# A one-core decoder layer: another order on VectorE around w_o, and two small fetches at another place

## The chip, the core and the metric

The kernel runs on one core of one Trainium2 chip. A core has five engines that run side by side, each through its own list of instructions in order, and that wait for one another by semaphores. TensorE (PE in the profile) does matrix products, and the loading of its stationary operand is shown beside it as PEld. VectorE (DVE) and ScalarE (ACT) do elementwise work, and read the results of TensorE from PSUM banks. GpSimd (POOL) does some elementwise work and starts some transfers. SyncE (SP) starts most transfers between the device's memory and the on-chip memory. The metric is device time in microseconds (us) for one launch.

## The reference

One pre-norm layer on 512 tokens of 1024 features, in float32. What matters here is the middle and the end of it:

```
merged = gates[0] * y_a + gates[1] * y_b + gates[2] * y_c      # y_c = ssd_mixer(...) @ w_c
x = x + merged @ w_o                                           # w_o is 1024 x 1024
u = rmsnorm(x, ln2_g)          # x * rsqrt(mean(x*x) + 1e-6) * ln2_g, row by row
h = causal_dwconv(u @ w_up, conv_w, conv_b)                    # w_up is 1024 x 5632, three taps
x = x + (silu(h[:, :2816]) * h[:, 2816:]) @ w_down
out = rmsnorm(x, final_g)
```

The norm ahead of the FFN needs a whole row of the new x before any of its 1024 features can be used, and every product of w_up needs the normed rows. The convolution's taps and bias (`ffn_conv_w`, `ffn_conv_b`) are needed as columns, one scalar for each feature.

## The kernel before

**Arithmetic.** Each float32 product is done as three products of a reduced format: an operand is split in a high part and a rest, `high` and `low`. For a weight tile, ScalarE casts the high part (`wh`, line 195) and VectorE subtracts it from the raw tile to get the rest (`wl`, line 217, the "weight sum" below is this instruction and its relatives on line 1377). `mm3` (line 238) then issues high by high, high by low and low by high.

**Jobs.** The work is a list of jobs (`program`), each with a weight tile to fetch (`fetch`, on SP), to cast (`cast`) and to split (`low`), and a `body` that issues the products. While the body of job n runs, job n+1's tile is split, job n+2's is cast and job n+3's is fetched. Small pieces of other work are generators in the list `running`; `step()` lets each of them go on by one `yield`, so where a `step()` stands in a body decides where such a piece stands in the lists of the engines. The lists of PE, ACT, DVE and POOL are in the order in which the Python code issues the instructions; that of SP is set by the framework.

**w_o.** `wo_group` computes `merged @ w_o` by seven products of half size in place of eight, so seven jobs named two, five, three, one, six, seven and four, in this order. Each job makes two products, one for each of two blocks of 128 rows, in two PSUM banks (`bank[0]`, `bank[1]`). Banks called A serve one, six, seven and four, banks called B two, five and three: a later job of the same banks adds onto what an earlier one left. So after each product `read(i)` has VectorE add the bank to a tile of x (line 1351, "a reading of a bank"), and the next job that adds onto this bank can't start its product before that reading. Job one finishes the left half of row blocks 0 and 1, job six their right half, job seven the left-out half of row blocks 2 and 3, and job four the rest of these.

**The norm.** Behind a reading stands either `first` or `then`. `first` (after one's readings, and after seven's) begins the norm of a row block with the half that is ready: the squares and their sum on ScalarE (line 439), two small VectorE instructions that make `v0` and `vh` from the sum (lines 463 and 1297), and the product with the norm's gain on GpSimd (line 464). `then` (after six's and four's readings) takes the other half: squares and a square root on ScalarE (line 473), a small VectorE instruction (line 478), and after a `yield` the reciprocal and its refinement on VectorE (lines 481 to 483), then the two halves of the normed rows `u`, one on VectorE (line 487), one on ScalarE (line 488). `norm_turn` transposes the normed rows on PE into PSUM (line 453, `uT`), and ScalarE and VectorE make the high part `uh` and the rest `ul` of them (lines 456 and 457). For row blocks 0 and 1 this last part runs as `rest(2)` in `running`; for row blocks 2 and 3 it is called from the first FFN jobs (`opening`, line 1543), which therefore start on row blocks 0 and 1 alone.

**Small tables.** `ff_cols` fetches the convolution's taps and bias as rows (three transfers on line 512), transposes them on PE (line 518, `fcol0p` and `fcol1p`) and copies the result with VectorE (line 519, `fcol`). It is called after job one (`i == 3`), and the PE and VectorE part runs at the third `step()` after it. The transposes of `ff_cols` and `norm_turn` take PSUM banks in turn from one set of four. ScalarE's square root needs a table that is loaded when the function is first used after another set (an ACT_TABLE_LOAD on line 473). `load_x1` fetches the norm's gain and some tiles of x ahead of the fourth of the four w_c jobs; `one_read` holds what follows one's readings, among it job four's weight sum (`total`, line 1377).

Of the kernel before, what the change touches and what calls it, by code (L numbers as in the profile page):

```python
# [10 lines left out]
F32 = mybir.dt.float32  # L11
F32R = mybir.dt.float32r
AF = mybir.ActivationFunctionType
OP = mybir.AluOpType
AX = mybir.AxisListType

P = 128
S = 512
D = 1024
KD = D // P  # L20
EPS = 1e-6
# [61 lines left out]
def trunk(ctx: ExitStack, tc, out, x, rel_bias, ln1_g, w_in, b_gate, w_a, pool_w, pool_scale, w_b,  # L83
# [3 lines left out]
    act, dve, pool, pe, sp = nc.scalar, nc.vector, nc.gpsimd, nc.tensor, nc.sync  # L87
# [5 lines left out]
    cpool = ctx.enter_context(tc.tile_pool(name="const", bufs=1))  # L93
# [12 lines left out]
    def T(name, dt=F32, shape=(P, S)):  # L106
        return big.tile(list(shape), dt, name=name, tag="t")
# [7 lines left out]
    def small(name, shape, dt=F32):  # L115
        return tiny.tile(list(shape), dt, name=name, tag="tiny")
# [4 lines left out]
    eps = cpool.tile([P, 1], F32, name="eps")  # L121


    waiting, running = [], []
# [38 lines left out]
    def after(n, it):  # L163
        for _ in range(n):
            yield
        yield from it
# [269 lines left out]
    def squares(eng, src, ss):  # L436
        junk = T("junk")
        if eng is act:
            act.activation(junk, src, AF.Square, accum_out=ss)
        else:  # L440
            dve.scalar_tensor_tensor(junk, src, 1.0, src, OP.mult, OP.mult, accum_out=ss)

    def grow(src):
        g = [T("grow") for _ in range(2)]
        for h in range(2):
            sp.dma_start(g[h], src[h * S:(h + 1) * S].partition_broadcast(P))
        return g

    def norm_turn(us, uh, ul, tb):
        for h in range(2):  # L450
            ps = SM("uT")
            for j in range(4):
                pe.transpose(ps[:, j * P:(j + 1) * P], us[h][:, j * P:(j + 1) * P], eye)
            pv = ps.rearrange("p (j t) -> p j t", j=4)
            hh = uh[:, 4 * h:4 * h + 4, tb * P:(tb + 1) * P]
            act.copy(hh, pv)
            dve.tensor_sub(ul[:, 4 * h:4 * h + 4, tb * P:(tb + 1) * P], pv, hh.bitcast(F32))

    def norm_early(t, g, h=0):

        ss, v0, xg = small("ss", [P, 1]), cpool.tile([P, 1], F32, name=f"v0_{len(V0)}"), T("xg")
        squares(act, t, ss)
        dve.tensor_scalar(v0, ss, 1.0 / D, EPS, OP.mult, OP.add)
        pool.tensor_tensor(xg, t, g[h], OP.mult)
        V0.append(v0)
        return v0, xg
# [788 lines left out]
    X1 = {}  # L1255
    nxt = {}
    late, late_split = [], []

    def load_x1():
        nxt["g2"] = grow(ln2_g[0])  # L1260
        for tb, h in ((0, 1), (1, 1), (2, 0), (3, 0)):
            t = X1[tb, h] = T("x1")
            sp.dma_start(t, x[tb * P:(tb + 1) * P, h * S:(h + 1) * S])

    def wo_group():
# [26 lines left out]

        def first(tb, h):
            half = 1 - h
            v0, xg = norm_early(X1[tb, half], nxt["g2"], half)
            vh = cpool.tile([P, 1], F32, name=f"vo{tb}")
            dve.tensor_scalar(vh, v0, -0.5, None, OP.mult)
            nxt[tb] = v0, vh, xg

        def then(tb, h):  # L1300
            if "uh" not in nxt:
                nxt["uh"] = upool.tile([P, KD, S], F32R, name="uh2", tag="uh")
                nxt["ul"] = upool.tile([P, KD, S], F32R, name="ul2", tag="ul")
            v0, vh, xg0 = nxt[tb]
            us = [T("u0"), T("u1")]
            it = norm_late(X1[tb, h], nxt["g2"], v0,
                           lambda: (us[h], (us[1 - h], xg0)), vh, h, True)
            next(it)

            def rest(n=1):  # L1310
                next(it, None)
                for _ in range(n):
                    yield
                norm_turn(us, nxt["uh"], nxt["ul"], tb)

            if tb < 2:
                running.append(rest(2))
            elif tb == 2:
                r2 = rest()
                next(r2)  # L1320
                late.append(r2)
            else:
                late.append(rest())
                for _ in late_split.pop(0):
                    pass
# [50 lines left out]
        def total(out, a, b, op=OP.add):  # L1376
            dve.tensor_tensor(out, a, b, op)
            return out

        def one_read(tb):  # L1380
            first(tb, 1)
            if tb == 0:
                total(four.raw, four.raw, W[2])

        two = job("A12", quarter(1, 0), None, B, (0, 0), apart=True, fresh=True)
        five = job(1, None, lambda: W[0], B, (1, 1), apart=True, fresh=True)
# [226 lines left out]
    def program():  # L1613
        yield from jobs_a(w_in, C_POOL, 8, uhk, ulk, KD, pool_evac)
        yield Call(lambda: waiting.append(rows_of_bias()))
        yield from v_jobs(0)
        yield Call(lambda: running.extend(after(3 * p, sums_of_u(p)) for p in (0, 1)))
        yield from qk_jobs(0)
        yield from pool_out_job()
        yield Call(lambda: attend(0))  # L1620
        yield Call(lambda: waiting.insert(3, ssd_prep()))
        gates = gate_seven(1)
        pair, residues_of_v = v_pair()
        groups = gates, pair, qk_sevens(1)
        for i, job in enumerate(branch_jobs(1, w_b, YB, 8, more=range(7))):
            if i == 1:
                yield Call(gates.load[0])
            if i == 2:
                yield Call(lambda: running.extend(after(2 * p - 4, sums_of_u(p)) for p in (2, 3)))
                yield Call(gates.load[1])  # L1630
                yield Call(gates.load[2])
            yield job
        yield Call(lambda: second_table())
        last = None
        for group, next_ in zip(groups, groups[1:] + (None,)):
            yield group.two
            if last:
                yield last.four
            last = group
            for i, job in enumerate(group.jobs):  # L1640
                if next_ and i >= 2:
                    yield Call(next_.load[i - 2])
                yield job
        xbc = jobs_a(w_in, C_XBC, 12, uhk, ulk, KD, xbc_evac)
        yield next(xbc)
        yield last.four
        yield Call(lambda: attend(1))
        yield Call(lambda: running.extend(after(2, f()) for f in (residues_of_v, residues_of_bias)))
        yield from xbc
        yield Call(ssd_start)  # L1650
        yield from qk_jobs(2)
        yield Call(lambda: attend(2))
        yield Call(lambda: fill([after(2, combine())]))
        yield from gate_jobs(0)
        many = {"a": branch_jobs(0, w_a, AO, 3), "g": gate_jobs(2),
                "Z": z_jobs(0), "z": z_jobs(1)}
        load, sums, group = wo_group()
        for token in MIX:
            if token == "w":
                yield Call(load)  # L1660
            elif token in many:
                yield next(many[token])
            else:
                yield Call(lambda i=int(token): waiting.append(y_norm(i)))
        yield Call(finish)
        for i, job in enumerate(branch_jobs(2, w_c, YT, 8, last=True)):
            if i == 1:
                yield Call(sums)
            if i == 3:
                yield Call(load_x1)  # L1670
            yield job
        for i, job in enumerate(group):
            yield job
            if i == 3:
                yield Call(ff_cols)
        loads, groups = zip(*(down_group(base) for base in range(0, KS, 8)))
        between = {}
        for group, ats in zip(groups, AT):
            for jobs_, at in zip(group, ats):
                between.setdefault(at, []).extend(jobs_)  # L1680
        for i, job in enumerate(up_jobs()):
            yield job
            for load, ats in zip(loads, AT):
                if i == ats[0] - 3:
                    yield Call(load)
            yield from between.get(i, ())
        yield Call(lambda: fin.setdefault("g", grow(final_g)))
        plain = down_jobs(0)
        yield next(plain)
        yield from between.get(2 * (KF // 2), ())  # L1690
        yield from plain
        yield from down_jobs(1)
# [22 lines left out]
    first = [MM("pa") for _ in range(4)]  # L1715
# [63 lines left out]
    for tb in range(2):  # L1779
        s0, s1, v, sq, r, rt = (small(n, [P, 1]) for n in ("s0", "s1", "v", "sq", "r", "rt"))  # L1780
# [25 lines left out]
    ss = row_squares(2, small("ss", [P, 4]), 2)  # L1806
# [36 lines left out]
    n = 0  # L1843
# [68 lines left out]
```

## Time and profile before

| what | us |
|---|---|
| median of 3 runs | 1023.51 (1023.18 to 1023.67) |
| profiled execution, its own time | 1024.06 |
| span of that execution in the trace | 1022.3 |
| PE busy | 1007.1 |
| DVE busy | 718.6 |
| ACT busy | 518.7 |
| POOL busy | 143.7 |

The profile's times count from the start of the span. Job one of w_o starts on PE at 633.17 us, the first FFN job at 664.28, and from 677.52 the FFN runs over all rows. A row of the timeline gives the start, the length, the engine, the line, the operation, the tiles written and read, the count of merged instructions, and in square brackets the engine's idle time before it and what ended that. PEclk is the clock that TensorE was granted, 1.00 being full speed.

### The profile page before, as it was taken

The page shows a single profiled execution, that of the slowest core. Times are in us where ns is not written, and L with a number is a line of the kernel's source. Part 1 is how long each engine was busy: PE and PEld are TensorE (multiplying, and loading weights), DVE is VectorE, ACT ScalarE, POOL GpSimd, SP SyncE. Part 2 cuts the span into 40 slices and gives each one's busy share as a digit, 9 for nine tenths or more (in the row PEclk, how much of TensorE's full clock was granted, in tenths as well). Part 3 has the DMA queues.
Part 4 walks back from the last instruction along what each step waited for, and adds up shares of the span by engine and source line. Part 5 has one row for each costly group of instructions (what it writes and reads, how often), then busy time and mean ns, then how long its engine had stood idle before and what let it go on. Part 6 is the DMA issues. An engine that isn't in the chain of part 4 may idle for free.

```text
span 1022.3 us, 13624 instructions
## 1 busy us (share of the span) xinstructions
PE 1007.1 (99%) x5378; PEld 858.1 (84%) x5378; DVE 718.6 (70%) x910; ACT 518.7 (51%) x877; POOL 143.7 (14%) x128
## 2 busy tenths in 40 slices
PE   8999999999999999999999999899999999999997
PEld 8898878999988888888888887698888888888885
DVE  6564768677757647667889688658778768685756
ACT  5433546564435476879567235554444444433434
POOL 1691000010000000000064501102111100111002
PEclk9999999999999999999999999999999999999999
DMA  8538222155253343552256346332232332321322
GB/s 269 169 100 210 95 72 76 57 150 167 93 183 107 90 126 102 145 142 86 83 166 166 113 145 162 129 118 89 95 112 83 99 107 82 125 83 42 124 103 83
DMA packets 114623, 121.26 MB, mean 119 GB/s; under 512 B 6499, under 2 KB 96166, under 8 KB 114559
## 3 DMA queue, kind: packets, MB, share of 16 engines
q1 hardware_dynamic: 111087, 114.81, 36.2%
q0 software_dynamic: 2880, 4.72, 2.7%
q8 instruction: 42, 0.69, 0.3%
q10 hardware_dynamic: 592, 0.86, 0.2%
q14 instruction: 22, 0.18, 0.1%
HBM read 116.58 MB, written 3.00 MB: 117 GB/s over the span
## 4 chain that ended last, share of the span: by engine, by line
PE 96%; DVE 2%; DMA 1%; ACT 1%; issue 0%; ACTq 0%; DVEq 0%
PE pa L238 36%; PE pu L238 22%; PE pb L238 10%; PE pd L238 7%; PE pqk L238 6%; PE pq L238 3%; PE pa L1760 2%; PE ps L786 1%; PE pu L1543 1%; PE ppw L238 1%; PE po L834 1%; PE pt L820 1%; PE py L1119 1%; DVE wl L217 1%; DMA xin<-in_x_dram 1%; PE pyo L1126 1%
## 5 line engine op out<-in xcount | busy, mean ns | idle before, releaser
L217 DVE TENSOR_TENSOR wl<-raw,wh 128x2048 fp32r<-128x2048 f32 (+3 forms) x87 | 202.7, 2330 | 47.6 <-ACT wh L195 33.9
L195 ACT CAST wh<-raw 128x1024 fp32r<-128x1024 f32 (+4 forms) x171 | 171.5, 1020 | 63.4 <-DVE raw L361 17.8
L1438 DVE SCALAR_TENSOR_TENSOR hc<-pu,fcol,hc 128x510 f32<-128x510 f32 x88 | 65.9, 749 | 56.4 <-ACT hc L1435 54.8
L238 PE MATMUL pa<-uh,wh 128*128 128x512 f32 (+1 forms) x368 | 88.8, 381 | 0.0
L238 PE MATMUL pa<-ul,wh 128*128 128x512 f32 (+1 forms) x368 | 86.8, 375 | 0.0
L238 PE MATMUL pa<-uh,wl 128*128 128x512 f32 (+1 forms) x368 | 86.8, 375 | 0.0
L238 PE MATMUL pu<-uh,wh 128*128 128x512 f32 (+1 forms) x352 | 83.5, 379 | 0.0
L238 PE MATMUL pu<-ul,wh 128*128 128x512 f32 (+1 forms) x352 | 83.5, 379 | 0.0
L238 PE MATMUL pu<-uh,wl 128*128 128x512 f32 (+1 forms) x352 | 83.5, 379 | 0.0
L238 PEld LDWEIGHTS pa<-ul,wh 128*128 128x128 f32 x368 | 66.7, 188 | 12.6
L238 PEld LDWEIGHTS pa<-uh,wl 128*128 128x128 f32 x368 | 66.7, 188 | 12.5
L238 PEld LDWEIGHTS pa<-uh,wh 128*128 128x128 f32 x368 | 65.4, 189 | 11.8
L238 PEld LDWEIGHTS pu<-uh,wl 128*128 128x128 f32 x352 | 64.2, 188 | 12.5
L238 PEld LDWEIGHTS pu<-ul,wh 128*128 128x128 f32 x352 | 64.2, 188 | 12.5
L238 PEld LDWEIGHTS pu<-uh,wh 128*128 128x128 f32 x352 | 64.1, 188 | 12.4
L1435 ACT ACTIVATE hc<-pu,fcol,fcol 128x512 f32<-128x512 f32 x40 | 31.2, 779 | 79.0 <-PE pu L238 79.0
L1443 POOL TENSOR_TENSOR hc<-hc 128x512 f32<-128x512 f32 x22 | 30.8, 1399 | 286.0 <-DVE hc L1438 225.8
L217 DVE TENSOR_TENSOR wl<-w,wh 128x2048 fp32r<-128x2048 f32 (+1 forms) x22 | 47.3, 2151 | 10.2 <-issue 4.6
L808 ACT ACTIVATE sb<-sb,nmls 128x128 f32<-128x128 f32 (+1 forms) x72 | 30.0, 418 | 31.7 <-DVE nmls L805 21.1
L195 ACT CAST wh<-w 128x1024 fp32r<-128x1024 f32 (+1 forms) x44 | 41.0, 971 | 4.8 <-PE pb L238 2.4
L1102 POOL TENSOR_TENSOR st<-st,dts 128x512 f32<-128x512 f32 x4 | 4.2, 1050 | 225.5 <-ACT st L1110 163.5
L1440 ACT ACTIVATE hc<-hc 128x512 f32<-128x512 f32 x22 | 13.9, 632 | 39.9 <-DVE hc L1438 39.9
(424 smaller groups left out, 1950.9 us busy)
## 6 DMA issues: line engine op xcount, KB each, us to landing
raw<-in_w_in_dram SPq DMA_DIRECT2D x24, 1024.0 KB
raw<-in_ffn_w_up_dram SPq DMA_DIRECT2D x22, 1024.0 KB
raw<-in_ffn_w_down_dram SPq DMA_DIRECT2D x8, 1024.0 KB
raw<-in_w_in_dram SPq DMA_DIRECT2D x14, 512.0 KB
raw<-in_w_in_dram SPq DMA_DIRECT2D x8, 768.0 KB
raw<-in_w_b_dram SPq DMA_DIRECT2D x4, 1024.0 KB
al<-ad SPq DMA_DIRECT2D x16, 256.0 KB
raw<-in_w_c_dram SPq DMA_DIRECT2D x4, 1024.0 KB
```

Source lines behind the costliest of these rows:

```text
L195: (other.tensor_copy if other and i else act.copy)(job.high[:, :, o], job.raw[:, :, o])
L217: (eng or dve).tensor_tensor(l[:, :, o], job.raw[:, :, o], h[:, :, o].bitcast(F32), OP.subtract)
L238: pe.matmul(ps, l, r, start=first and n == 0, stop=last and n == total - 1, skip_group_check=onto)
L786: pe.matmul(pss[i][:, o:o + w * P], q[r, n * P:(n + 1) * P], k[r, kb * P:(kb + w) * P], start=True, stop=True)
L808: act.activation(sb[:, off:off + w * P], sb[:, off:off + w * P], AF.Exp, bias=nm[:, n, h:h + 1], accum_out=ls[:, n, h:h + 1])
L820: pe.transpose(pt[:, o:o + P], sb[:, o:o + P], eye)
L834: pe.matmul(po[DH * hh:DH * hh + DH, n * P:(n + 1) * P], V[g, kb + i][:, (2 * c + hh) * DH:(2 * c + hh + 1) * DH], probs[2 * c + hh, nb][: ...
L1435: act.activation(t, ps, AF.Identity, bias=ff["c1"][:, ff["b"] + m:ff["b"] + m + 1], scale=fw(2, m))
L1438: dve.scalar_tensor_tensor(t[:, sh:], ps[:, :S - sh], fw(k, m), t[:, sh:], OP.mult, OP.add)
L1440: act.activation(t, t, AF.Silu)
L1443: pool.tensor_tensor(a, a, t, OP.mult)
L1760: pe.matmul(first[2 * n + j][:, lo:hi], a[:, k, j * P:(j + 1) * P], b[:, k, lo:hi], start=a is wh and b is uh and k == 0, stop=a is wl and ...
```

## The change

Four places are touched.

1. `load_x1` gets a square root of one column on ScalarE, whose result nobody reads. The table of the square root is so loaded during w_c, and not at the first square root of the norm.
2. `first` issues only the squares and the product with the gain. The two small VectorE instructions that make `v0` and `vh` go to `then`, behind the reading of the other half. In `one_read`, job four's weight sum goes ahead of `first`.
3. For row block 1, `rest(2)` becomes `after(1, rest(1))`: the reciprocal and what follows on VectorE and ScalarE come one `step()` later, the transposes stay at the same `step()`.
4. `ff_cols` is called after job five (`i == 1`), not after job one.

In the engines' lists: on PE the two transposes of `fcol` go from behind seven's first product to between one's two products, and nothing else moves. On VectorE, between one's first reading and four's second, the order becomes: reading (one), weight sum for four, the two `fcol` copies, reading (one), seven's weight sum, reading (six), the three small instructions of row block 0, reading (six), the three of row block 1, reciprocal to `u` of row block 0, the same of row block 1, four's weight sum, reading (seven), `ul` twice, reading (seven), `ul` twice, reading (four). On ScalarE the square root with its table load is added behind a cast of `merged` (`mgh`) that is made during the last w_c job, and the `u` of row block 0 comes behind the squares and the root of row block 1. On SP the three `fcol` transfers go ahead of the first fetch of w_up and of the second fetch of w_down; before, they stood behind both. GpSimd's list is the same.

```
     def load_x1():
         nxt["g2"] = grow(ln2_g[0])
+        act.activation(small("sq", [P, 1]), eps, AF.Sqrt)
...
         def first(tb, h):
             half = 1 - h
-            v0, xg = norm_early(X1[tb, half], nxt["g2"], half)
-            vh = cpool.tile([P, 1], F32, name=f"vo{tb}")
-            dve.tensor_scalar(vh, v0, -0.5, None, OP.mult)
-            nxt[tb] = v0, vh, xg
+            ss, xg = cpool.tile([P, 1], F32, name=f"so{tb}"), T("xg")
+            squares(act, X1[tb, half], ss)
+            pool.tensor_tensor(xg, X1[tb, half], nxt["g2"][half], OP.mult)
+            nxt[tb] = ss, xg
...
-            v0, vh, xg0 = nxt[tb]
+            ss, xg0 = nxt[tb]
+            v0, vh = (cpool.tile([P, 1], F32, name=f"{n}{tb}") for n in ("va", "vo"))
+            dve.tensor_scalar(v0, ss, 1.0 / D, EPS, OP.mult, OP.add)
+            dve.tensor_scalar(vh, v0, -0.5, None, OP.mult)
...
             if tb < 2:
-                running.append(rest(2))
+                running.append(rest(2) if tb else after(1, rest(1)))
...
         def one_read(tb):
-            first(tb, 1)
             if tb == 0:
                 total(four.raw, four.raw, W[2])
+            first(tb, 1)
...
             yield job
-            if i == 3:
+            if i == 1:
                 yield Call(ff_cols)
```

## The prediction

> **What bounds the kernel now.** I read the page's busy times first, then what TensorE waited for over the whole run, then the timelines of TensorE and VectorE around w_o, and last the granted clock there.
>
> ```profile
> PE 1007.1 (99%) x5378; PEld 858.1 (84%) x5378; DVE 718.6 (70%) x910; ACT 518.7 (51%) x877; POOL 143.7 (14%) x128
> ```
>
> TensorE is the bound: 1007.1 of 1022.3 us. A change that leaves its products alone can only win what TensorE waits, or runs slowly. All its waits of the run, longest first, are these (engine, what it waited for, us, times, longest):
>
> ```profile
> PE uT L453 <- DVE fcol L519: 3.5, 1, 3.5
> ...
> PE pb L238 <- DVE x L1351: 1.0, 1, 1.0
> PE uT L453 <- ACT u L488: 0.4, 1, 0.4
> PE pb L238 <- DVE wl L217: 0.3, 1, 0.3
> ```
>
> The two left out (DVE diag and DVE ones) are at the start of the run. These four, 5.2 us, all lie in w_o, and after 657 us TensorE waits for nothing up to its last product. So whatever time TensorE gains there shifts all that follows. Its timeline:
>
> ```profile
> 633.17 1.98 PE L238 MATMUL pb<-wh,m 128*128 128x512 f32 x8
> ...
> 638.61 1.07 PE L238 MATMUL pb<-wh,sah 128*128 128x512 f32 x4
> ...
> 645.25 1.16 PE L238 MATMUL pb<-wh,sbh 128*128 128x512 f32 x4 [1.04 <-DVE x L1351]
> ...
> 648.10 0.27 PE L518 MATMUL fcol0p<-eye,fcol0r 128*128 128x128 f32 x1
> 648.30 0.26 PE L518 MATMUL fcol1p<-eye,fcol1r 48*128 48x48 f32 x1
> 648.99 1.09 PE L453 MATMUL uT<-eye,u 128*128 128x128 f32 x8 [0.43 <-ACT u L488]
> 649.84 1.17 PE L238 MATMUL pb<-wh,sbh 128*128 128x512 f32 x4
> ...
> 656.29 1.06 PE L453 MATMUL uT<-eye,u 128*128 128x128 f32 x8 [3.46 <-DVE fcol L519]
> 657.12 1.82 PE L238 MATMUL pb<-wh,mgh 128*128 128x512 f32 x4
> ...
> 661.54 1.09 PE L238 MATMUL pb<-wh,mgh 128*128 128x512 f32 x4
> ...
> 668.12 1.04 PE L453 MATMUL uT<-eye,u 128*128 128x128 f32 x8
> 668.91 2.15 PE L1543 MATMUL pu<-uh,wl 128*128 128x256 f32 x16
> ```
>
> Job one begins at 633.17 and six at 638.61: a job of 24 products takes 5.44 us, half a job 2.72. By that six ends at 644.05 and seven starts 1.20 late, at 645.25. A second loss is hidden in four: its first half runs from 657.12 to 661.54, 4.42 us instead of 2.72. The granted clock tells why (columns: stretch, its length, busy time and count of PE, PEld, DVE, ACT, POOL, then PEclk, DMA share, GB/s):
>
> ```profile
> 650.57:653.98 3.41, 2.26 (x10) 1.51 (x9) 3.25 (x5) 2.62 (x4) 0.00 (x0) 1.00 0.00 0
> 653.98:657.39 3.41, 1.09 (x9) 1.13 (x10) 2.59 (x9) 1.68 (x4) 1.27 (x1) 1.00 0.55 170
> 657.39:660.80 3.41, 3.41 (x9) 2.67 (x8) 2.26 (x6) 1.69 (x4) 1.28 (x1) 0.50 0.41 137
> ```
>
> The clock was halved for 3.41 us, from 657.39 to 660.80. In the 3.41 us before that TensorE had been idle for 3.41 - 1.09 = 2.32 us; in the 3.41 us before those, for 1.15 us, with no such effect. So a third idle did nothing here, and two thirds cost 4.42 - 2.72 = 1.70 us.
>
> VectorE sets these waits by the order of its list. The parts of it that carry the sum:
>
> ```profile
> 636.18 0.68 DVE L1351 TENSOR_TENSOR x<-x,pb 128x512 f32<-128x512 f32 x1
> ...
> 637.91 2.47 DVE L1377 TENSOR_TENSOR raw<-raw,w 128x2048 f32<-128x2048 f32 x1
> 640.31 0.68 DVE L1351 TENSOR_TENSOR x<-x,pb 128x512 f32<-128x512 f32 x1
> ...
> 644.43 0.68 DVE L1351 TENSOR_TENSOR x<-x,pb 128x512 f32<-128x512 f32 x1
> 645.90 0.16 DVE L478 SCALAR_TENSOR_TENSOR v<-ss,vo 128x1 f32<-128x1 f32 x1 [0.79 <-ACT junk L439]
> ...
> 657.37 0.68 DVE L1351 TENSOR_TENSOR x<-x,pb 128x512 f32<-128x512 f32 x1
> ...
> 659.32 1.29 DVE L457 TENSOR_TENSOR ul<-uT,uh 128x512 fp32r<-128x512 f32 x2
> 661.74 0.69 DVE L1351 TENSOR_TENSOR x<-x,pb 128x512 f32<-128x512 f32 x1 [1.14 <-PE pb L238]
> ...
> 663.54 0.16 DVE L481 RECIPROCAL r<-sq 128x1 f32<-128x1 f32 x1 [0.17 <-ACT sq L473]
> ...
> 664.19 0.75 DVE L487 SCALAR_TENSOR_TENSOR u<-x,rt,grow 128x512 f32<-128x512 f32 x1
> 664.86 0.68 DVE L1351 TENSOR_TENSOR x<-x,pb 128x512 f32<-128x512 f32 x1
> 666.33 0.16 DVE L478 SCALAR_TENSOR_TENSOR v<-ss,vo 128x1 f32<-128x1 f32 x1 [0.79 <-ACT junk L439]
> 666.41 2.29 DVE L217 TENSOR_TENSOR wl<-raw,wh 128x2048 fp32r<-128x2048 f32 x1
> ```
>
> Before the small `v` VectorE idles 0.79 us for ScalarE's squares. `first` has such a `v` too (line 463), and the next weight sum or reading is queued behind it.
>
> **The change part by part.** I walk through the new lists from 633.17, where both kernels are still alike.
>
> *The fcol fetch and transposes.* They come to stand between one's two products, at 635.89. Between zero (they are no new work) and 0.89 (from 648.10 to 648.99, a wait included); the start of one to the next is 0.20, so I take 0.35 for both. One then ends at 638.96, six at 644.40. The two copies on VectorE cost 0.31 together (they stand ahead of a reading there, and take the place of a wait for `v`).
>
> *Weight sums and readings first.* One's first reading stays at 636.18 to 636.86. Four's sum follows at once: 2.40 to the next start (637.91 to 640.31), so 639.19; the copies, 639.50; one's second reading, 0.61, to 640.11; seven's sum, of the same size, 2.40 again, to 642.51; six's first reading until 643.19. This is what seven's first product waited for. It is there before 644.40, so the 1.20 us wait goes, and seven runs from 644.40 to 647.12.
>
> *The early square root.* It is hidden if ScalarE idles where it is put.
>
> ```profile
> 613.61 0.41 ACT L1222 CAST m<-yo 128x256 fp32r<-128x256 f32 x1 [3.58 <-DVE yo L1247]
> ...
> 645.88 1.28 ACT L473 ACT_TABLE_LOAD   x1
> 647.18 0.29 ACT L473 ACTIVATE sq<-ss,v 128x1 f32<-128x1 f32 x1
> ```
>
> Load and root are 1.28 + 0.29 = 1.57 us, put among w_c's casts ahead of the first row here, before which ScalarE idles 3.58. Cost zero there, at most 1.57 if that cover is gone. At 645.88 the load goes out of the norm's way. It isn't a term of its own: the sum below has no load in it.
>
> *The norm of blocks 0 and 1, regrouped.* Six's second product ends at 644.40, and its reading starts 0.20 later, as 661.74 stands to 661.54: at 644.60. From a reading to `v` is 1.47 (644.43 to 645.90), with `va` and `vo` in the idle 0.79. `v` takes 0.08 to the next start (666.33 to 666.41), so the reciprocal of block 0 starts at 646.15. Reciprocal to `u` is 0.65, and `u` 0.67 to the next start (663.54, 664.19, 664.86): 1.32 for a block, 2.64 for both, to 648.79. Block 0's `u` ends at about 647.6 on both engines, so its transposes on TensorE wait from 647.12 to 647.66, 0.54 where 0.43 stood. With 0.85 for them (648.99 to 649.84) and 2.72, seven ends at 651.23. Block 1's `u` is ready by 648.9 and the banks are free, so the 3.46 us wait goes: transposes to 652.07, and four starts there, 5.05 us earlier than now. Without the long wait the clock should stay up: first half of four to 654.79.
>
> *What is late next.* VectorE goes on at 648.79 with four's sum, 2.20 to the next start (a 2.29 us sum without GpSimd beside it), to 650.99. Then come two rounds of reading, squares, casts and `ul`: one such round is 659.32 + 1.29 - 0.08 - 657.37 = 3.16 us. So seven's second reading starts at 654.15 and ends at 654.83; four's second product wants its bank and waits 0.2 us, to 655.0. Four's first reading starts at 657.31. From that reading to the end of the weight sum that the FFN's first job needs is 666.41 + 2.29 - 661.74 = 6.96 us: 664.27. TensorE ends four at 657.72, takes 3.84 for two FFN parts (as from 664.28 to 668.12) and 0.79 for transposes, and is there at 662.35. It waits 2.0 us, until 664.33. That part started at 668.91 before.
>
> ```profile
> 623.21 0.38 SPq L1491 DMA_DIRECT2D w<-in_ffn_w_down_dram  x1
> 632.24 0.37 SPq L182 DMA_DIRECT2D raw<-in_ffn_w_up_dram  x1
> ...
> 640.91 0.46 SPq L512 DMA_DIRECT2D fcol0r<-in_ffn_conv_w_dram  x1
> ```
>
> *SP.* The three small fetches now follow the issue at 623.21, so at 623.7. They pass the w_up fetch, which waits for a buffer until 632.24 anyway and loses nothing. The second w_down fetch waits for four's sum and goes earlier with it.
>
> **The sum.** Gone: 1.20 (seven), 3.46 and about 0.3 (second transposes, slow restart), 1.70 (half clock), 0.1 (slower products after a wait). New: 0.2 and 2.0. Net 668.91 - 664.33 = 4.6 us, and nothing behind it gives it back, since TensorE has no wait there. The profiled execution took 1024.06 us, 1.76 over its span; it would take 1019.5. The median of the runs is 0.55 lower, 1023.51, so the forecast is 1018.9.
>
> **The rivals.**
>
> *The clock is halved after the new wait.* A 2.0 us wait is 59% of 3.41 if it falls into one such stretch, between the 34% that did nothing and the 68% that halved the clock. Price: 1.70 us, since TensorE has no slack after 664.33. Gain 2.9, time 1020.6. Against it: part of the wait may fall into the next stretch. The Trainium skill (TensorE: Matmul & The Clock Gate, Part 1 and the table under "Why this matters for your kernels") says that the clock falls back after a whole idle window of about 3.4 us, and asks only that gaps over about 3 us be avoided. By that rule this rival doesn't happen and 1018.9 stands; but here a stretch that was one third busy was enough, so the row goes against the rule as stated.
>
> *The chain on VectorE is shorter than I add up.* If ScalarE's and VectorE's rounds lose their idle pieces, the 2.0 us wait doesn't come: gain 6.6, time 1016.9. Against it: each round contains squares, casts and subtractions that follow one another.
>
> *The gain is given back.* If TensorE, ahead by 4.6, meets a fetch or a cast that was just in time, the time stays at 1023.5. Against it: no wait of TensorE in the FFN, and the fetches are let go by weight sums that move along with it.
>
> *Slower: the fcol rows arrive late.* TensorE now stops inside one for them, and VectorE has their copies ahead of a reading and of seven's sum, so all that follows is held. They have 635.89 - 623.7 = 12.2 us to land, behind a weight fetch; before, issued at 640.91 behind the second such fetch, they had landed by 648.10, in at most 7.2 us. To eat the gain they must land after 640.5, 16.8 us after issue; at 645 the time would be 1028.
>
> **How the numbers follow.** Forecast 0.50, half clock 0.30, shorter chain 0.06, given back 0.09, slower 0.05. Two tenths of a per cent, 2 us, is about what a measurement tells from no change here; the first three are faster by more. So faster 0.86, same 0.09, slower 0.05. The range is from 1017.8 (the forecast with the chain 1 us shorter) to 1021.4 (half clock, and the chain 0.8 us longer).
>
> **What the changed profile would show.** Seven's first product without a wait, at about 644.4. The second `uT` without one. Four's first half in 2.7 us at clock 1.00. `fcol0p` near 635.9 without a wait. A wait of about 2 us for `wl` ahead of `pu<-uh,wl`, then the clock at 1.00 or 0.50 for 3.41 us: this decides between the first two cases. The table load near 607. Wrong would be a wait of TensorE for `fcol0r`, for ScalarE in five or three, or a new one in the FFN.

## The result, and the profile after

The changed kernel takes 1019.20 us (median of 6 runs, 1018.85 to 1019.97); the kernel before took 1024.08 in the runs beside it (6 runs, 1023.18 to 1027.85). The ratio is 0.9947, with a 95% interval of 0.9931 to 0.9963. On another chip, later, it was 1019.21 against 1023.52, ratio 0.996 (0.9948 to 0.9973). So it is faster by about half a per cent, 4.3 to 4.9 us, and the forecast was 1018.9.

One sentence ahead of the prediction is wrong: the `after(1, rest(1))` of the third edit is for row block 0, not 1 (`rest(2) if tb else ...`). The order of VectorE's list given there is right, and the prediction worked with it.

The busy times on the page of the changed kernel:

```profile
PE 1005.1 (99%) x5378; PEld 856.6 (84%) x5378; DVE 718.1 (71%) x910; ACT 518.4 (51%) x878; POOL 147.7 (15%) x128
```

TensorE has lost 2.0 us of busy time with the same 5378 products, most of it in the slow first half of four (4.42 us before, 2.83 now). Its waits now, longest first (engine, what it waited for, us, times, longest):

```profile
PE uT L1781 <- DVE diag L1793: 2.8, 2, 1.6
PE pu L1547 <- DVE wl L217: 1.8, 1, 1.8
PE pa L1723 <- DVE ones L1714: 1.1, 1, 1.1
PE uT L453 <- ACT u L488: 0.4, 1, 0.4
PE pb L238 <- DVE wl L217: 0.3, 1, 0.3
```

Diag and ones are the start of the run, as before. Of the 3.5 us for `fcol` and the 1.0 for a reading nothing is left, and one wait is new, 1.8 us for a weight sum in the FFN's first job. TensorE's timeline around w_o, changed kernel:

```profile
633.44 1.98 PE L238 MATMUL pb<-wh,m 128*128 128x512 f32 x8
...
636.16 0.27 PE L518 MATMUL fcol0p<-eye,fcol0r 128*128 128x128 f32 x1
636.36 0.26 PE L518 MATMUL fcol1p<-eye,fcol1r 48*128 48x48 f32 x1
636.55 2.11 PE L238 MATMUL pb<-wh,m 128*128 128x512 f32 x8
...
639.41 1.07 PE L238 MATMUL pb<-wh,sah 128*128 128x512 f32 x4
...
644.85 1.07 PE L238 MATMUL pb<-wh,sbh 128*128 128x512 f32 x4
...
648.08 1.09 PE L453 MATMUL uT<-eye,u 128*128 128x128 f32 x8 [0.35 <-ACT u L488]
...
651.78 1.03 PE L453 MATMUL uT<-eye,u 128*128 128x128 f32 x8
652.57 1.17 PE L238 MATMUL pb<-wh,mgh 128*128 128x512 f32 x4
...
655.40 1.10 PE L238 MATMUL pb<-wh,mgh 128*128 128x512 f32 x4
...
662.00 1.04 PE L453 MATMUL uT<-eye,u 128*128 128x128 f32 x8
664.78 2.18 PE L1547 MATMUL pu<-uh,wl 128*128 128x256 f32 x16 [1.75 <-DVE wl L217]
```

Seven starts without a wait at 644.85, the second transposes come without one at 651.78, and four's first half takes 655.40 - 652.57 = 2.83 us where it took 4.42. Then TensorE stands before `pu<-uh,wl`. Job one starts 0.27 us later than before in this execution (633.44 against 633.17), and between the runs of this study it starts anywhere from 632.28 to 633.44, with the change and without it. So the measure from here on is the start of this `pu<-uh,wl` less the start of job one. It was 668.91 - 633.17 = 35.74 before and is 664.78 - 633.44 = 31.34 now: 4.40 less. Behind it nothing has moved: from there to the end of the span it is 1022.3 - 668.91 = 353.4 us before, and 1018.2 - 664.78 = 353.4 now.

What TensorE waits for is at the end of VectorE's list; the rows of it that carry the chain:

```profile
637.04 2.29 DVE L1381 TENSOR_TENSOR raw<-raw,w 128x2048 f32<-128x2048 f32 x1
...
645.05 0.69 DVE L1355 TENSOR_TENSOR x<-x,pb 128x512 f32<-128x512 f32 x1 [0.87 <-PE pb L238]
...
646.61 0.16 DVE L481 RECIPROCAL r<-sq 128x1 f32<-128x1 f32 x1
...
649.23 2.28 DVE L217 TENSOR_TENSOR wl<-raw,wh 128x2048 fp32r<-128x2048 f32 x1
...
662.44 2.29 DVE L217 TENSOR_TENSOR wl<-raw,wh 128x2048 fp32r<-128x2048 f32 x1
```

From six's second reading (645.05), which TensorE sets, to the weight sum that the FFN's first job needs (662.44 to 664.73) VectorE waits for TensorE nowhere: only for ScalarE, inside the rounds of reading, squares, casts and `ul`.

And the granted clock (columns as in the prediction: stretch, length, busy time and count of PE, PEld, DVE, ACT, POOL, PEclk, DMA share, GB/s), in the stretch with the wait and the next:

```profile
663.16:666.57 3.41, 1.79 (x15) 1.79 (x16) 2.77 (x5) 2.60 (x5) 0.00 (x0) 1.00 0.14 34
666.57:669.98 3.41, 3.41 (x31) 3.41 (x30) 3.40 (x3) 0.46 (x1) 0.00 (x0) 1.00 0.79 274
```

TensorE was idle for 3.41 - 1.79 = 1.62 us of the first, 48%, and the clock stayed at 1.00 in the second.

### The profile page after: what moved, and what is told of

Read it like the earlier page. It is cut to its first block, busy times and chain, and to the rows that moved or that the text cites. A ratio compares the mean times of both kernels' runs of the same rounds, so it can differ in the third digit from the quotient of the medians.

```text
span 1018.2 us, 13635 instructions
## 1 busy us (share of the span) xinstructions
PE 1005.1 (99%) x5378; PEld 856.6 (84%) x5378; DVE 718.1 (71%) x910; ACT 518.4 (51%) x878; POOL 147.7 (15%) x128
## 4 chain that ended last, share of the span: by engine, by line
PE 96%; DVE 2%; DMA 1%; ACT 0%; issue 0%; ACTq 0%; DVEq 0%
PE pa L238 36%; PE pu L238 23%; PE pb L238 10%; PE pd L238 7%; PE pqk L238 6%; PE pq L238 3%; PE pa L1764 2%; PE ps L786 1%; PE ppw L238 1%; PE po L834 1%; PE pt L820 1%; PE py L1119 1%; PE pu L1547 1%; DMA xin<-in_x_dram 1%; DVE wl L217 1%; PE pyo L1126 1%
```

## The experiments

**The theories.** Theory A, from the prediction: two lists run against each other, TensorE's products and waits, and VectorE's chain that ends in the weight sum for `pu<-uh,wl`. The later of the two sets the time. Theory B: each part of the change is worth the wait that it answers, and the parts add up. In the kernel before the two lists were nearly level: the weight sum there ended at 666.41 + 2.29 = 668.70, and TensorE came at 668.91, after 3.46 us of waiting and 1.70 of half clock. By A a part that frees TensorE alone gains little, though that wait is the longest: only what VectorE's own list waits for the late TensorE, as the 1.14 us ahead of its reading at 661.74.

### The small tables alone

The kernel before, with `ff_cols` called after job five and nothing else.

```
             yield job
-            if i == 3:
+            if i == 1:
                 yield Call(ff_cols)
```

> Only the earlier call of ff_cols, on the kernel before. Theory A (the gain is the chain of VectorE and ScalarE work from six's readings to the weight sum that the FFN's first job waits for): the 3.46 us wait and the half clock go, but the chain still has its waits for the squares in it, so TensorE stops at that weight sum and the FFN's third part starts only about 1.4 us earlier; the time falls by 1.4 us, 0.14%. Theory B (each part is worth the wait it answers): 3.5 us of wait and 1.7 us of half clock go, 5.2 us, 0.5%.

Measured: 1022.25 us (11 runs, 1022.09 to 1022.94) against 1023.31, ratio 0.9988 (0.9979 to 0.9997); 1.1 us of gain where B has 5. TensorE's timeline:

```profile
652.61 1.03 PE L453 MATMUL uT<-eye,u 128*128 128x128 f32 x8
654.80 1.19 PE L238 MATMUL pb<-wh,mgh 128*128 128x512 f32 x4 [1.16 <-DVE x L1351]
...
667.36 2.18 PE L1543 MATMUL pu<-uh,wl 128*128 128x256 f32 x16 [1.69 <-DVE wl L217]
```

and the row of VectorE's that the last one waits for:

```profile
665.02 2.29 DVE L217 TENSOR_TENSOR wl<-raw,wh 128x2048 fp32r<-128x2048 f32 x1
```

The 3.46 us wait for `fcol` is gone, and so is the half clock. In their place stand 1.16 us for a reading and 1.69 for the weight sum. Job one started at 632.79, so the measure is 34.57, 1.17 less than before. The weight sum starts 665.02 - 632.79 = 32.23 us after job one, where it was 666.41 - 633.17 = 33.24: VectorE no longer waits 1.14 us for four's first product, about as much as its list gains. The largest wait in the profile and its half clock, some 5 us together, were worth 1.1 by themselves.

### VectorE's order alone

The kernel before, with the second part of the change only: `first` issues the squares and the gain, the small instructions for `v0` and `vh` go to `then`, and four's weight sum stands ahead of `first`.

```
         def one_read(tb):
-            first(tb, 1)
             if tb == 0:
                 total(four.raw, four.raw, W[2])
+            first(tb, 1)
...
```

The edits of `first` and `then` are as in the diff ahead of the prediction.

> Only the new place of the small VectorE instructions and of four's weight sum, on the kernel before: the root's table, the turn of block 0 and ff_cols stay where they were. Theory A: nearly the whole gain, 3.9 us of 4.4 to the start of the FFN's third part, with the wait of the second transposes for fcol still there (about 1.7 us) and without a half clock. Theory B: only the 1.2 us wait ahead of seven goes, the 3.5 us wait and the half clock stay.

Measured: 1020.33 us (1019.65 to 1020.87) against 1023.31, ratio 0.9968 (0.9956 to 0.9981); 3.0 of the 4.3 to 4.9 us. That is 0.9 short of the expectation. The rows of TensorE and of the clock:

```profile
652.90 1.27 PE L453 MATMUL uT<-eye,u 128*128 128x128 f32 x8 [2.02 <-DVE fcol L519]
653.82 2.05 PE L238 MATMUL pb<-wh,mgh 128*128 128x512 f32 x4
...
658.14 1.07 PE L238 MATMUL pb<-wh,mgh 128*128 128x512 f32 x4
...
665.49 2.16 PE L1546 MATMUL pu<-uh,wl 128*128 128x256 f32 x16
```

```profile
650.20:653.62 3.42, 1.41 (x11) 0.97 (x10) 2.67 (x4) 2.50 (x5) 0.99 (x1) 1.00 0.11 17
653.62:657.03 3.41, 3.41 (x12) 2.73 (x10) 1.95 (x4) 1.95 (x6) 1.47 (x2) 0.50 0.83 290
```

The wait for `fcol` was 2.02 us, not 1.7, and with it TensorE was idle for 59% of a stretch. The clock was halved in the next, which the expectation had left out, and four's first half took 658.14 - 653.82 = 4.32 us. `pu<-uh,wl` starts 665.49 - 633.04 = 32.45 us after job one, without a wait: 3.29 earlier than before, where 3.9 was expected. VectorE's list:

```profile
645.24 0.16 DVE L481 RECIPROCAL r<-sq 128x1 f32<-128x1 f32 x1 [1.45 <-ACT sq L473]
...
663.01 2.29 DVE L217 TENSOR_TENSOR wl<-raw,wh 128x2048 fp32r<-128x2048 f32 x1
```

TensorE is the later one here, but only by 0.2 us: the weight sum ends at 663.01 + 2.29 = 665.30. So the 1.6 us that the half clock takes from TensorE explain only a small part of the 1.1 us by which this kernel is behind the whole change (32.45 against 31.34). Most of that is in VectorE's list, where the reciprocal of row block 0 still waits 1.45 us for the root and its table load. The experiment "Both of these" below has the same wait and no half clock. Its reciprocal comes 644.83 - 632.64 = 12.19 us after job one, as here (12.20), and its `pu<-uh,wl` at 32.12; by that the half clock costs this kernel some 0.3 us. A is right on which part carries the gain: 3.29 of the 4.40 us.

### The early root left out

The changed kernel without the square root ahead of w_o.

```
         nxt["g2"] = grow(ln2_g[0])
-        act.activation(small("sq", [P, 1]), eps, AF.Sqrt)
```

> The changed kernel without the early square root. Theory A: no difference, 0.0 us; the load falls between the squares of block 0 and those of block 1, where ScalarE idles 1.46 us in the changed kernel. Theory B: 1.3 us slower, as much as the load takes, since it stands in the norm's way again.

Measured: 1019.02 us (1018.89 to 1019.43), ratio 0.9957 (0.9944 to 0.9969), and the measure is 663.83 - 632.48 = 31.35. Nothing is lost, although the table load stands in the norm again, 1.28 us from 643.05 on.

### Block 0's later turn undone

The changed kernel with `rest(2)` for both row blocks.

```
-                running.append(rest(2) if tb else after(1, rest(1)))
+                running.append(rest(2))
```

> The changed kernel with rest(2) for both row blocks 0 and 1. Theory A: 0.4 us faster, since block 0's reciprocal to u fits in the 0.87 us in which VectorE waits for six's second product, and the chain behind it ends earlier. Theory B: slower by some tenths of a us, since six's second reading stands behind this work again.

Measured: 1018.75 us (1018.31 to 1018.97), ratio 0.9952 (0.9939 to 0.9966); the measure is 663.79 - 632.95 = 30.84, 0.50 less than the changed kernel's, 0.1 more than expected. The later turn costs half a microsecond: block 0's reciprocal to `u` then stand behind the second reading, and VectorE idles 0.87 us ahead of that reading (the row at 645.05 above).

### Both of these

Each of the two last edits alone loses nothing. Together they do.

> The changed kernel with both block 0's later turn undone and the early square root taken out; each of the two alone was tried before, and cost nothing. Theory C (both answer the same 1.28 us table load: either the load is out of the norm's way, or VectorE has another reading to do while it lasts): with both gone the reciprocal of row block 0 waits about 1.45 us for the root, as in the kernel with the new order alone, and all that follows on VectorE comes 1.28 us later than where the turn alone is undone: pu<-uh,wl starts 32.1 us after job one, with a wait of about 1.3 us for a reading ahead of four's second product and one of 1.7 us for the weight sum, neither long enough to halve the clock; time 1020.0 us, 1.28 over the 1018.75 of that kernel. Theory D (the early root is worth nothing wherever the turn stands): pu<-uh,wl at 30.8 us and 1018.75 us. At about 1022 the clock would have been halved after one of the two waits.

Measured: 1019.79 us (1019.64 to 1020.19) against 1023.42, ratio 0.9964 (0.995 to 0.9977). VectorE's timeline of this kernel:

```profile
643.22 0.16 DVE L478 SCALAR_TENSOR_TENSOR v<-ss,vo 128x1 f32<-128x1 f32 x1 [0.54 <-ACT junk L439]
644.83 0.16 DVE L481 RECIPROCAL r<-sq 128x1 f32<-128x1 f32 x1 [1.45 <-ACT sq L473]
```

The reciprocal waits 1.45 us for the root, and the measure is 664.76 - 632.64 = 32.12, 1.28 more than with the turn alone undone: the length of the load. In time it is 1.04 us (1019.79 against 1018.75, on two chips). The waits of TensorE came out as 0.76 for the reading ahead of four and 1.69 for the weight sum, the clock stayed at 1.00. So theory C holds: the early root and block 0's later turn answer the same 1.28 us, the one by taking the load away, the other by giving VectorE something else to do meanwhile. With the later turn the early root is worth nothing; without it, 1.28.

### The small tables late again

The changed kernel with `ff_cols` after job one, as before the change.

```
-            if i == 1:
+            if i == 3:
                 yield Call(ff_cols)
```

> The changed kernel with ff_cols called after job one again, as before the change. Theory A: 0.3 us faster: the copies go back to a place where VectorE idles 1.26 us, the second transposes wait about 0.7 us for them, and the wait of about 1.75 us for the weight sum takes that up. Theory B: 3.5 us slower, the wait is back, or 5.2 us with the half clock.

Measured: 1018.58 us (1018.22 to 1019.35) against 1023.67, ratio 0.9953 (0.9941 to 0.9966); the measure is 664.14 - 633.31 = 30.83, 0.51 less than the changed kernel's where 0.3 was expected. What the early place removes is 0.51 us of wait for `fcol` here, hidden under a 1.10 us wait for the weight sum; what it costs is in front of the chain.

Taken together: the second edit carries most of the gain. Beside it the early root and block 0's later turn are two answers to the same table load, and one of them is enough. With these in place the early call of `ff_cols` costs 0.51 us, though alone it gained 1.17. The second edit with one of those two and nothing else was not run.

### The weight sum ahead of four's second reading

The changed kernel, with the weight sum of the FFN's first job, and the cast and the fetch behind it, called one reading earlier.

```
                 next(r2)
                 late.append(r2)
-            else:
-                late.append(rest())
                 for _ in late_split.pop(0):
                     pass
+            else:
+                late.append(rest())
```

> The changed kernel with the weight sum of the FFN's first job, and the cast and fetch behind it, ahead of four's second reading. Theory A: the 1.75 us wait goes down to some 0.4 us, a new one of about 0.5 us stands at the next such sum; 1.0 us faster. Rival: the wait moves whole to the next sum or cast, and the time stays.

Measured: 1017.96 us (1017.71 to 1019.01), ratio 0.995 (0.9937 to 0.9963). The first `pu<-uh,wl` starts 662.08 - 632.28 = 29.80 us after job one with 0.20 of wait. What counts is the second one of the same job, for rows 2 and 3, since the norm of row block 3 now comes later:

```profile
669.22 2.17 PE L1547 MATMUL pu<-uh,wl 128*128 128x256 f32 x16 [0.25 <-DVE wl L217]
```

It starts 36.94 us after job one; in the changed kernel it was 671.43 - 633.44 = 37.99. So 1.05 us are gained, as expected, and the time follows (1.2).

### The three together, and the tables later still

The last kernel with the turn undone, `ff_cols` at `i == 3`, and in `opening` the next weight sum (`rest[0]`) ahead of row block 2's transposes and `ul` (`late.pop(0)`); and the same with `ff_cols` after job six, at `i == 4`.

```
                 product(ws[0], ul2, 1)
-                next(late.pop(0), None)
                 next(rest[0], None)
+                next(late.pop(0), None)
                 product(ws[1], uh2, 2)
```

> The changed kernel with the early weight sum, the next weight sum ahead of block 2's ul, block 0's turn undone and ff_cols late. Theory A: no wait over 0.6 us is left between job seven and the FFN, 2.2 us faster than the changed kernel. Rival: as for the early sum alone, 1 us or less.

> The version that looked best, once more beside the changed kernel. Theory A (the chain on VectorE from six's readings to the weight sum): its pu<-uh,wl starts 29.6 us after job one, and the second one of rows 2 and 3 1.8 us earlier than in the changed kernel, so the time is 1.8 us below it, about 6.4 below the kernel before. If it is below by less than 1 us, the start of a product in one trace isn't worth as much in the time.

> As the version that looked best, with the fcol fetch called one job later, so that its two transposes come between four's two products and its copies into idle time of VectorE. Theory A: the last wait left around w_o, 0.73 us of uT for the fcol copies, goes, and TensorE comes to pu<-uh,wl 0.7 us earlier; the weight sum is there 0.1 to 0.4 us later than that, since the chain on VectorE loses at most the 0.31 us of the two copies. Net 0.3 to 0.6 us less than that version. Theory B (each wait is worth its own length): 0.7 us less. If the time is the same, the chain isn't shortened and the wait only moves to the weight sum; if it is more, the copies are in the chain's way at the new place too.

> The changed kernel once more, so that the two versions below have it on the same chip. Both theories: about 4.6 us below the kernel before, half a per cent; the third product of the first FFN job's rows 0 and 1 (pu<-uh,wl) starts 31.3 us after job one, behind a wait of about 1.75 us for the weight sum.

Measured: 1017.26 us (1017.07 to 1018.62) against 1023.67, ratio 0.9943 (0.993 to 0.9957), and again 1017.26 (1017.08 to 1017.64) against 1023.52, ratio 0.9938 (0.9924 to 0.9952). On that chip the changed kernel took 1019.21 (1018.91 to 1020.51), and the version with the tables later still 1017.15 (1016.87 to 1017.49), ratio 0.9937 (0.9925 to 0.9949). Both versions lie 2 us below the change, with no run in common. The second `pu<-uh,wl` starts 36.21 us after job one in the one and 35.94 in the other, 1.8 and 2.0 less than in the change (37.98 there). The first had been expected to gain 2.2; 0.73 us of wait for the `fcol` copies, which come later with the tables, had not been seen. Their difference of 0.27 is just under what was expected and too small for these times. TensorE's rows of the last version:

```profile
654.18 0.27 PE L518 MATMUL fcol0p<-eye,fcol0r 128*128 128x128 f32 x1
...
661.25 1.04 PE L453 MATMUL uT<-eye,u 128*128 128x128 f32 x8
662.31 2.17 PE L1547 MATMUL pu<-uh,wl 128*128 128x256 f32 x16
```

The list of TensorE's waits has nothing left from w_o on but the 0.3 us for a weight sum that the kernel before has too. The weight sum of this row ends at 662.25. With the 0.79 us that the transposes take to the next start in the kernel before (668.12 to 668.91), TensorE could have been there at 662.04: the two lists are level to within 0.3 us.

### What halves the clock

The prediction's first rival hung on how long TensorE must idle. The changed kernel with an added hold after each of the 20 later FFN jobs: a transpose, a copy and 0 to 8 small multiplications on VectorE, and a second transpose that waits for them. The layer's own work is unchanged.

```
+    def hold(n):
+        ps, t = MM("hold"), T("hold")
+        pe.transpose(ps[:, :P], eye, eye)
+        dve.tensor_copy(t[:, :P], ps[:, :P])
+        for _ in range(n % 5):
+            dve.tensor_tensor(t[:, P:2 * P], t[:, :P], t[:, :P], OP.mult)
+            dve.tensor_tensor(t[:, :P], t[:, P:2 * P], t[:, P:2 * P], OP.mult)
+        ps = MM("hold")
+        pe.transpose(ps[:, :P], t[:, :P], eye)
...
+                    hold(2 * p + half)
```

> The changed kernel with a hold at the end of each of the 20 later FFN jobs: TensorE transposes a constant tile, VectorE copies it and multiplies it zero to eight times, and TensorE transposes the result, so that TensorE idles for about 0.5 to 3.5 us in each of 20 places. It asks at which idle share of a stretch of 3.41 us the clock is halved for the next. Share theory: some share between 34% and 68% decides, and the stretches are at fixed multiples of 3.41 us, so a hold of 2 us halves the clock or not by where it falls. Rule of a wholly idle stretch: no hold under 3.41 us halves the clock.

Measured: 1154.73 us in one run. TensorE idled for 88.3 us in the 20 holds. They were longer than planned, 2.53 to 6.58 us each in place of 0.5 to 3.5, and fell at many places of a stretch, so that stretches of many shares came up. The stretches are cut here where the clock changed in this trace; all changes lie a multiple of 3.413 us apart.

```profile
977.39:980.81 3.42, 1.44 (x7) 0.89 (x5) 1.21 (x2) 0.78 (x1) 0.00 (x0) 1.00 0.00 0
980.81:984.22 3.41, 2.13 (x6) 1.77 (x7) 2.50 (x5) 1.56 (x2) 0.00 (x0) 0.50 0.01 2
984.22:987.63 3.41, 3.41 (x10) 2.64 (x9) 3.06 (x2) 0.00 (x0) 0.00 (x0) 0.50 0.00 0
...
1093.45:1096.86 3.41, 1.51 (x8) 0.96 (x6) 1.13 (x2) 1.97 (x3) 0.00 (x0) 1.00 0.00 0
1096.86:1100.28 3.42, 0.69 (x4) 0.64 (x5) 3.35 (x6) 2.49 (x4) 1.56 (x1) 1.00 0.00 0
```

In the first stretch TensorE was idle for 1.98 us, 58%, and the next one ran at 0.50. In the one from 1093.45 it was idle for 1.90 us, 56%, and the next one ran at 1.00. In all the traces here no stretch at full clock with at most 56% idle was followed by a half one, and each inside the run with 58% or more was. The first rows show one thing more: a stretch at half clock that was itself 38% idle (980.81) was followed by another at half clock, so a wait there doubles the price. Two holds of the same length show that it isn't the length of the wait:

```profile
753.15 0.33 PE L1541 MATMUL hold<-eye,hold 128*128 128x128 f32 x1 [2.86 <-DVE hold L1536]
...
960.60 0.48 PE L1541 MATMUL hold<-eye,hold 128*128 128x128 f32 x1 [2.86 <-DVE hold L1536]
```

```profile
748.70:752.11 3.41, 1.59 (x8) 1.03 (x6) 1.76 (x3) 1.89 (x3) 0.17 (x1) 1.00 0.00 0
752.11:755.53 3.42, 2.38 (x11) 1.99 (x12) 3.42 (x4) 0.12 (x1) 1.30 (x1) 1.00 0.02 5
...
956.91:960.33 3.42, 0.83 (x5) 0.39 (x3) 1.81 (x4) 2.66 (x4) 0.15 (x1) 1.00 0.00 0
960.33:963.74 3.41, 3.14 (x8) 2.56 (x9) 3.30 (x3) 1.87 (x3) 1.15 (x1) 0.50 0.00 0
```

The first lies with 1.82 us in one stretch and 1.04 in the next, and halves nothing. The second lies nearly whole in one stretch, where TensorE idles for 76%, and the next ran at 0.50. A stretch need not be wholly idle either. So the clock went by the share of a stretch, and in these traces the border lies between 1.90 and 1.98 us of 3.41. The Trainium skill (TensorE: Matmul & The Clock Gate, Part 1) gives the window as 3413 ns, running freely; the spacing of the changes here agrees with it.

## Why the prediction was right

Times after job one's start, predicted and measured, so that the 0.27 us of a later start drop out:

| step | predicted | measured |
|---|---|---|
| six starts | 5.79 | 5.97 |
| seven starts, no wait | 11.23 | 11.41 |
| first `uT` | 14.49 | 14.64 |
| four starts, no wait before its transposes | 18.90 | 19.13 |
| four's second half | 21.83 | 21.96 |
| six's second reading | 11.43 | 11.61 |
| weight sum for `pu<-uh,wl` starts | 28.81 | 29.00 |
| `pu<-uh,wl` starts | 31.16 | 31.34 |

**The waits that go.** All three went as said: seven's 1.20, the second transposes' 3.46 and the half clock's 1.70. That they are not worth their sum was in the forecast too, as the new wait; the experiment with the small tables alone shows it, where 5 us of removed wait and slow clock gave 1.1.

**The new wait.** From 661.98 + 2.29 on VectorE a wait of 2.0 us was foretold, from the start that TensorE could have had to the start it got. Measured that way it is 664.78 - (662.00 + 0.79) = 1.99. VectorE's chain from six's second reading to the weight sum was worked out as 17.38 us from rows of before, and took 662.44 - 645.05 = 17.39. That isn't luck: its parts came out to within 0.05 us each, such as 2.62 for 2.64 (the two blocks from the reciprocal to `u`) and 3.15 and 3.14 for two rounds of 3.16.

**The mis-sized term.** The gain is 4.40 in place of 4.58, and the missing 0.18 stands in the table from its first row on. It is the step "*The fcol fetch and transposes*": 0.35 us for both. They took 636.55 - 636.16 = 0.39, and the product behind them 639.41 - 636.55 = 2.86 instead of 2.72, since the products begin slower after transposes. The step costs 0.53, and it lies ahead of the chain, so the chain carries it to the end. The experiment with the tables late again measures the same from the other side, 0.51.

**Smaller ones.** The 0.2 us wait of four's second product did not come. TensorE got there 0.34 us later than worked out, counted from job one (the mis-sized term, and the same slow beginning in seven's second half and four's first), and the reading that it needs only 0.16 later. Two weight sums put at 2.40 us to the next start took 2.20 and 2.33, which counts for nothing, since VectorE waits 0.87 us behind them. The low end of the range should have been 1017.9 by the words beside it. The added work on ScalarE was free:

```profile
607.07 0.62 ACT L1227 CAST mgh<-yo 128x512 fp32r<-128x512 f32 x1 [2.71 <-DVE yo L1247]
607.71 1.28 ACT L1261 ACT_TABLE_LOAD   x1
609.00 0.20 ACT L1261 ACTIVATE sq<-eps 128x1 f32<-128x1 f32 x1
...
613.89 0.41 ACT L1222 CAST m<-yo 128x256 fp32r<-128x256 f32 x1 [2.70 <-DVE yo L1247]
```

ScalarE still idles 2.70 us ahead of the cast before which it idled 3.58. From the first cast of `m` ahead of the load (at 603.01; 602.73 before) to job one it is 30.43 us, and it was 30.44.

That the early root "isn't a term of its own" is right for this kernel only: 1.28 us hang on it where block 0 has its old turn.

**The rivals.** *Half clock after the new wait* did not happen. Its working put 2.0 us into one stretch, 59%, but the 2.0 were from start to start, while the share goes by idle time, which is 1.75 from the end of the transposes. Even all of it in one stretch would be 51%, under the 56% that did nothing; in the kernel without the early root it did fall whole into one stretch (1.75 us from 662.05 on), and the next ran at 1.00. The mechanism is real: the kernel with the order alone ran into it, with 59%. A chance of 0.30 was not too much for what the rows of before showed, 34% and 68%. Of the rule of the Trainium skill (TensorE: Matmul & The Clock Gate, Part 1), by which a whole idle window brings the clock down, these traces bear out what it gives here, but not the rule itself: 58% of a stretch was enough. *Given back* is excluded by the 353.4 us behind `pu<-uh,wl`, equal in both. *The late fcol rows* did not come either: they were issued from 623.96 on and their transposes at 636.16 didn't wait. *The shorter chain* is what the later versions made by hand, and the time fell by 2 us as a chain shorter by 1.8 to 2.0 asks.

## What to carry to other kernels

Before a long wait is removed, look at which other list would have come there next, and when: here 5 us of wait and slow clock of one engine hid a list of another that was only 0.2 us shorter, and removing them alone gave 1.1. Two edits that each seem to cost nothing when undone can stand in for one another, so undo them together before one is dropped as useless. A step put ahead of the critical chain costs its full length, even where the same step had been hidden a few microseconds later. And when an experiment falls short, compare the ends of both lists before the shortfall is put down to what is plain to see: with the order alone that was the half clock, but most of the 1.1 us to the whole change was in VectorE's list.

## What the runs showed that was not expected

The granted clock of TensorE was halved for 3.41 us after each stretch of 3.41 us inside the run in which it had idled for 1.98 us or more, and in no case after 1.90 us or less. At half clock, 38% of idle time was enough to keep it there for another stretch.

The first four products behind transposes take 1.17 us (the row at 652.57) where others take 1.07, and a whole product there 2.83 to 2.86 instead of 2.72. Before the change four products behind a wait took 1.16 (645.25). The prediction counted 0.1 us for such a slow beginning behind a wait, and nothing behind transposes; what in the engine causes it was not tried.
